# Weight sums and first operands of the feed-forward network moved into the first half of the output projection

## The chip, the cores and the metric

The kernel runs on one core of one Trainium2 chip. The metric is the device time of one execution in microseconds. The core has five engines that run side by side, each through its own queue in order: TensorE (PE, with its weight loads as PEld), VectorE (DVE), ScalarE (ACT), GpSimd (POOL) and SyncE (SP). SP issues most transfers, POOL the others. A difference of under 0.2% (1.45 us here) is about what a measurement of this kernel cannot tell from no change.

## The reference

One decoder layer over 512 tokens of width 1024, all in float32. What matters here are its last two parts:

```python
    merged = jax.nn.sigmoid(gate_a) * y_conv + jax.nn.sigmoid(gate_b) * y_attn
    x = x + merged @ w_out[l]                          # output projection, 1024 x 1024
    h2 = rmsnorm(x, g_ffn[l])
    gu = h2 @ w_ffn_in[l]                              # 1024 x 5632
    x = x + (jax.nn.silu(gu[..., :D_FF]) * gu[..., D_FF:]) @ w_ffn_out[l]
```

Ahead of them stand the input projection, a convolution branch and a forgetting attention (the "mixers").

## The kernel before, in words

Every float32 product is made as three products of split operands: hi·hi, hi·lo and lo·hi, where hi is a cast to the type fp32r (made on ACT) and lo is the rest (a subtraction on DVE, or an accumulating transfer from POOL).

**Output projection.** `n_group` (L263) runs twice, for columns 0 to 511 (`go[0]`) and 512 to 1023 (`go[1]`). Each has four weight chunks of 512 KB, here called chunk 0 to 3 and chunk 4 to 7. Each chunk meets the four token blocks of 128 (t = 0 to 3). A chunk is loaded by SP into `wraw` (3 buffers), cast by ACT into `whi`, and its rest made by DVE into `wlo` (3 buffers each). `go[0]` goes chunk by chunk. `go[1]` takes chunk 4 for all four token blocks and then, for each token block, chunks 5, 6 and 7 (`tail=3`), so that the blocks are done one after the other. `o_done` adds each result to the residual `x1` on DVE and takes the sum of squares on ACT (`junk`). Behind chunk 4's second token block stand the two products of `gain2`, which wait until the first residuals have been added.

**Feed-forward network.** The first product of the network, `w_ffn_in`, is made by a Strassen-Winograd scheme: for each of 11 column groups m there are seven products (m, p), p = 1 to 7, of 128x1024 quarter blocks of weights with operands of the normalised activations. Weight quarters are loaded by SP as `wA` tiles, 512 KB each; from four of them the sums S1 to S4 are made on DVE (`f_sum`, S1 in a tile `wS`, the others in place in `wA`). `w_hi` and `w_lo` make the split `wh` and `wl`. `seq` is the order of the products: (0,1), (0,2), (1,1), (1,2), (0,5), (0,6), (1,5), (0,7), (1,6), (0,4) and so on; products (m,1) and (m,2) need plain quarters, (m,5), (m,6) and (m,7) need sums. A list `todo` says at which step of `seq` each sum and split is made.

**Activations.** `norm2(t)` runs for each token block t: mean square (`ms`), the power on POOL (`rs`), two scalings on DVE (`h`), transposes on PE, copies on ACT (`hr`), and then the splits `bh` (ACT) and `bl` (DVE). For t = 2 and 3 it also makes the Winograd operands: T1 = hr - hr for products (m,5), T2 for (m,6), T3 for (m,7), T4 for (m,4). These steps are handed out by `tokens` between the first products.

**What sets the order.** The program is written in one order by small cooperative threads (`Line.spawn`, `Line.tick`, one tick for each token block of a chunk); each engine works through its own instructions in that order. A thread `prep_first` makes the splits of the first four products and, for m = 0, the four sums and the split of (0,5). It is started ahead of `go[1]`.

**Memory.** A pool `side` holds the mixers' tiles. It is released (`side.release()`) between `go[0]` and `go[1]`, and a new pool takes its place, with 22 buffers `f4` of 4 KB a partition for the network. A transfer into a new tile waits for the last use of whatever lay there. The first eight `wA` loads (m = 0 and 1) are written behind that release, so that in SP's queue they stand behind the last chunk of the output projection.

Of the kernel before, what the change touches and what calls it, by code (L numbers as in the profile page):

```python
# [35 lines left out]
def hybrid_layer(ctx, tc, x, g_mix, w_in, b_forget, w_dw, b_dw, g_ln, b_ln, w_conv_out,  # L36
# [129 lines left out]
    def add_group(w, kt, nk, c0, n, pair=None):  # L166

        first = len(plan)
        for k0 in range(0, kt, nk):
            plan.append(dict(w=w, k0=k0, nk=nk, c0=c0, n=n, pair=pair))  # L170
        return range(first, len(plan))
# [10 lines left out]
    go = [add_group(w_out, KT, 2, c * 512, 512) for c in range(2)]  # L182
# [12 lines left out]
    def load(i):  # L195
        while len(loaded) <= min(i, len(plan) - 1):
            d = plan[len(loaded)]
            n = d["n"]
            cols = n * (1 if d["pair"] is None else 2)
            raw = wp.tile([P, d["nk"], cols], F32, tag="raw", bufs=RAW, name="wraw")  # L200
            for at, c0 in halves(d):
                nc.sync.dma_start(raw[:, :, at:at + n], w_rows(d, c0))
            loaded.append(raw)

    def prepare(i):
        while len(ready) <= min(i, len(plan) - 1):
            load(len(ready))
            raw = loaded[len(ready)]
            loaded[len(ready)] = None
            hi = wp.tile(list(raw.shape), F32R, tag="whi", bufs=3, name="whi")  # L210
            lo = wp.tile(list(raw.shape), F32R, tag="wlo", bufs=3, name="wlo")
            A.copy(hi, raw)  # L212
            if len(ready) in by_dma:

                d = plan[len(ready)]
                A.activation(lo, raw, AF.Copy, scale=-1.0)  # L216
                for at, c0 in halves(d):
                    G.dma_start(lo[:, :, at:at + d["n"]], w_rows(d, c0), accum_op=ALU.add)  # L218
            else:
                V.tensor_tensor(lo, raw, hi.bitcast(F32), op=ALU.subtract)  # L220
            ready.append((hi, lo))

    def chunk(i):
        prepare(i + 2)
        load(i + 2 + RAW)
        d = plan[i]
        return ready[i][0], ready[i][1], d["k0"], d["nk"]

    def mm3(o, l_hi, l_lo, r_hi, r_lo, first, last):
        T.matmul(o, l_hi, r_hi, start=first, stop=False)  # L230
        T.matmul(o, l_hi, r_lo, start=False, stop=False)
        T.matmul(o, l_lo, r_hi, start=False, stop=last)
# [26 lines left out]
    def n_group(group, l_of, done, tail=1, accs=acc):  # L259


        n = plan[group[0]]["n"]
        bank = [accs(n) for _ in range(NT)]  # L263
        k_end = plan[group[-1]]["k0"] + plan[group[-1]]["nk"] - 1

        def one(ch, t):
            hi, lo, k0, nk = ch
            for kk in range(nk):
                l_hi, l_lo = l_of(k0 + kk, t)
                mm3(bank[t], l_hi, l_lo, hi[:, kk, :], lo[:, kk, :], k0 + kk == 0, k0 + kk == k_end)  # L270

        body, last = group[:len(group) - tail], group[len(group) - tail:]
        for i in body:
            ch = chunk(i)
            for t in range(NT):
                one(ch, t)
                Line.tick()
        prepare(last[0] + 2)
        load(last[0] + 2 + RAW)
        chs = [ready[i] + (plan[i]["k0"], plan[i]["nk"]) for i in last]  # L280
        todo = [(t, ch) for t in range(NT) for ch in chs]
        for t, ch in todo:
            one(ch, t)
            if t == NT - 1 and (tail == 1 or ch is not chs[-1]):
                prepare(last[0] + 3 + [c is ch for c in chs].index(True))
            if ch is chs[-1]:
                done(t, bank[t])
            Line.tick()
# [54 lines left out]
    def half(tl, c):  # L343
        return tl[:, c * 512:c * 512 + 512]

    def mean_sq(dst, tl, c):

        junk = wk(BF16, name="junk")
        A.activation(junk, half(tl, c), AF.Square, scale=D ** -0.5, accum_out=dst[:, c:c + 1])
# [489 lines left out]
    norm_th = [None] * NT  # L839

    def o_done(c):
        def done(t, b):
            V.tensor_tensor(half(x1[t], c), half(x1[t], c), b, op=ALU.add)
            mean_sq(ms2[t], x1[t], c)
            if c == 0 and t == 2:
                Line.spawn(gain2(), 4)
            if c == 1:
                norm_th[t] = Line.spawn(norm2(t), 1, order=-t)
        return done

    def gain2():
        for b_ in gain_bcast(row, mx):
            g_bc2.append(slot(name="gffn")[:, :S])
            A.copy(g_bc2[-1], b_)
        yield 0

    m_l = lambda k, t: (merged[k][0][:, t * P:(t + 1) * P], merged[k][1][:, t * P:(t + 1) * P])
    n_group(go[0], m_l, o_done(0), accs=mx)
    Line.join(*m_ths)
    side.release()  # L860

# [15 lines left out]
    def f4(dt=F32, name="f4"):  # L877
        return side.tile([P, KH, 256], dt, tag="f4", bufs=22, name=name)
# [25 lines left out]
    def f_sum(m, key):  # L904
        if key == "S1":
            wq[m, key] = f4(name="wS1")
            V.tensor_tensor(wq[m, key], wq[m, "A21"], wq[m, "A22"], op=ALU.add)
            return
        a, b, o = {"S2": ("S1", "A11", "A11"), "S3": ("A11", "A21", "A21"), "S4": ("A12", "A11", "A12")}[key]
        V.tensor_tensor(wq[m, o], wq[m, a], wq[m, b], op=ALU.subtract)  # L910
# [11 lines left out]
    def w_hi(m, p, alloc=wp4):  # L922
        hi = alloc(F32R, "wh")
        A.copy(hi, wq[m, SRC[p]])  # L924
        ops_.setdefault((m, p), [None, None])[0] = hi

    def w_lo(m, p, alloc=wp4):
        hi, lo = ops_[m, p][0], alloc(F32R, "wl")
        ops_[m, p][1] = lo
        V.tensor_tensor(lo, wq[m, SRC[p]], hi.bitcast(F32), op=ALU.subtract)  # L930
# [11 lines left out]
    def plan_for(m, p, lead, fn, *args):  # L942
        if (m, p) in at:
            todo[max(at[m, p] - lead, 0)].append((fn, args))
# [129 lines left out]
    def prep_first():  # L1074

        yield 0
        for m, p, alloc in ((0, 1, raw4), (0, 2, f4), (1, 1, f4), (1, 2, f4)):
            w_hi(m, p, alloc)
            w_lo(m, p, alloc)
            yield 2  # L1080
        f_sum(0, "S1")
        w_hi(0, 5, raw4)
        yield 1
        f_sum(0, "S3")
        f_sum(0, "S2")
        yield 1
        f_sum(0, "S4")
        w_lo(0, 5, f4)

    def one(n):  # L1090
        product(*seq[n])
# [30 lines left out]
    for m in range(NP):  # L1122
        if m > 1:
            plan_for(m, 2, 5, w_neg, m, 2)
            plan_for(m, 2, 2, w_hi, m, 2)
            plan_for(m, 1, 2, w_hi, m, 1)
            plan_for(m, 1, 2, w_lo, m, 1)
        plan_for(m, 4, 5, w_neg, m, 4)
        plan_for(m, 4, 2, w_hi, m, 4)
        if m > 0:  # L1130
            plan_for(m, 5, 4, f_sum, m, "S1")
            plan_for(m, 5, 4, f_sum, m, "S3")
            plan_for(m, 5, 3, f_sum, m, "S2")
            plan_for(m, 5, 3, f_sum, m, "S4")
        for p in (5, 6, 7, 3):
            if (m, p) != (0, 5):
                plan_for(m, p, 2, w_hi, m, p)
                plan_for(m, p, 2, w_lo, m, p)
    loads = {4: [(2, "A11")], 5: [(2, "A12")], 7: [(2, "A21")], 8: [(2, "A22")], 11: [(3, "A12")], 12: [(3, "A11")]}
    for m in range(2, NP):  # L1140
        loads[at[m, 6] - 2] = [(m + 1, "A21"), (m + 1, "A22")]
        loads[at[m, 7] - 2] = [(m + 2, "A12")]
        loads[at[m, 4] - 2] = [(m + 2, "A11")]

    first_th = Line.spawn(prep_first(), 1)
    n_group(go[1], m_l, o_done(1), tail=3)
    Line.join(first_th, norm_th[0], norm_th[1])
    n2, n3 = (lambda: Line.step(norm_th[2])), (lambda: Line.step(norm_th[3]))
    tokens = {1: (n3, n2, n2), 2: (n3, n3, n2), 3: (n3, n2), 4: (n3, n2), 5: (n3,), 6: (n2, n3)}
    for n in range(NS):  # L1150
# [55 lines left out]
```

## Time and profile before

| | |
|---|---|
| time, median of 3 runs | 724.87 us (723.6 to 725.2) |
| the profiled execution's own time | 724.91 us |
| its span | 723.1 us |
| PE busy | 700.1 us (97%) |
| DVE busy | 461.9 us (64%) |
| ACT busy | 375.0 us (52%) |
| POOL busy | 132.7 us (18%) |
| moved by transfers | 92.13 MB |
| mean granted TensorE clock | 0.994 |

The span is the time from the first to the last instruction in the profile; 1.8 us of the execution lie around it. "Busy" for PE includes time in which matmuls overlap. An engine that waits is shown with the work that released it.

### The profile page before, as it was taken

To read this page: it belongs to the slowest core of one execution; us is meant where nothing else is said; L and a number is where in the kernel's file an instruction comes from. 1 tells how busy PE (TensorE), PEld (TensorE's weight loads), DVE (VectorE), ACT (ScalarE), POOL (GpSimd) and SP (SyncE) were. 2 spreads that over 40 slices of the span, in tenths; PEclk is the share of its full clock that TensorE was granted. 3 is DMA by queue.
4 is the path that set the end of the run, shared out by engine and by line. 5 is a ranking of instruction groups with operands and counts; after the bars stand their busy time and mean duration, and the time that the engine had idled before them with its cause. 6 is when DMAs were issued, how large, how long until landed. Compare 5 with 4: busy or idle time off the path is not lost.

```text
span 723.1 us, 10723 instructions
## 1 busy us (share of the span) xinstructions
PE 700.1 (97%) x4264; PEld 616.7 (85%) x4264; DVE 461.9 (64%) x718; ACT 375.0 (52%) x595; POOL 132.7 (18%) x154
## 2 busy tenths in 40 slices
PE   7999999899999999999887999999999999999997
PEld 5988889778888888887687999999999988888886
DVE  5589968988844567465767666766776664333333
ACT  6423645568877675535366555655556553222320
POOL 1301158633343210400100111111010100000000
PEclk9999999999999999999998999999999999999999
DMA  8438997246556612258003777666677553233203
GB/s 261 98 101 184 181 199 153 73 110 137 121 108 127 145 59 88 89 205 259 1 26 64 176 172 147 158 155 149 154 160 160 88 140 123 88 93 112 87 30 116
DMA packets 67126, 92.13 MB, mean 127 GB/s; under 512 B 3282, under 2 KB 46290, under 8 KB 67076
## 3 DMA queue, kind: packets, MB, share of 16 engines
q1 hardware_dynamic: 48100, 66.11, 30.4%
q0 software_dynamic: 18976, 25.35, 22.0%
q8 instruction: 33, 0.54, 0.3%
q14 instruction: 17, 0.14, 0.1%
HBM read 89.34 MB, written 2.10 MB: 126 GB/s over the span
## 4 chain that ended last, share of the span: by engine, by line
PE 83%; DVE 9%; ACT 4%; issue 1%; DMA 1%; SPq 0%; POOL 0%; ACTq 0%; POOLq 0%; DVEq 0%
PE acc L147 55%; PE mx L147 29%; DVE cv L147 2%; DVE wA L147 1%; DVE x L147 1%; DVE wl L147 1%; ACT wh L924 1%; ACT whi L212 1%; DVE bl L147 1%; DVE wlo L147 1%; DMA x<-in_x_dram 1%; DVE scr L147 1%; DVE h L147 0%; DVE kn L147 0%; DVE hr L147 0%
## 5 line engine op out<-in xcount | busy, mean ns | idle before, releaser
L147 DVE SCALAR_TENSOR_TENSOR cv<-apad,prm,cv 128x512 f32<-128x512 f32 x120 | 87.0, 794 | 0.0
L212 ACT CAST whi<-wraw 128x1024 fp32r<-128x1024 f32 (+1 forms) x52 | 54.4, 1049 | 56.5 <-PE acc L147 35.8
L147 PE MATMUL acc<-hT_hi,whi 128*128 128x512 f32 (+1 forms) x208 | 75.5, 384 | 0.9 <-ACT hT_hi L77 0.7
L147 PE MATMUL acc<-hT_lo,whi 128*128 128x512 f32 (+1 forms) x208 | 73.0, 370 | 0.0
L147 PE MATMUL acc<-hT_hi,wlo 128*128 128x512 f32 (+1 forms) x208 | 72.7, 368 | 0.0
L147 DVE TENSOR_TENSOR wdl<-wd,wdh 128x1024 fp32r<-128x1024 f32 x22 | 27.0, 1225 | 70.1 <-ACT wdh L77 70.1
L147 DVE TENSOR_TENSOR wl<-wA,wh 128x1024 fp32r<-128x1024 f32 x46 | 55.6, 1223 | 22.5 <-ACT wh L924 22.5
L924 ACT CAST wh<-wA 128x1024 fp32r<-128x1024 f32 x66 | 68.0, 1045 | 0.0
L147 PE MATMUL acc<-bl,wh 128*128 128x256 f32 x352 | 57.2, 285 | 4.6 <-DVE bl L147 4.6
L77 ACT CAST wdh<-wd 128x1024 fp32r<-128x1024 f32 x22 | 23.0, 1048 | 74.6 <-PE mx L147 68.3
L920 POOL DMA_DIRECT2D wl<-in_w_ffn_in_dram x20 | 25.7, 1287 | 186.5 <-DVE act L147 91.3
L147 PE MATMUL acc<-bh,wh 128*128 128x256 f32 x352 | 56.9, 284 | 2.1 <-ACT bh L979 0.8
L147 PE MATMUL acc<-bh,wl 128*128 128x256 f32 x352 | 57.2, 285 | 0.2 <-DVE wl L147 0.2
L147 DVE TENSOR_TENSOR wlo<-wraw,whi 128x1024 fp32r<-128x1024 f32 x28 | 34.3, 1224 | 31.6 <-ACT whi L212 30.6
L147 PEld LDWEIGHTS acc<-bl,wh 128*128 128x128 f32 x352 | 48.7, 192 | 5.0 <-DVE bl L147 5.0
L147 PEld LDWEIGHTS acc<-bh,wh 128*128 128x128 f32 x352 | 48.2, 190 | 3.0 <-ACT bh L979 1.2
L147 PEld LDWEIGHTS acc<-bh,wl 128*128 128x128 f32 x352 | 48.6, 191 | 0.5 <-DVE wl L147 0.5
L218 POOL DMA_DIRECT2D wlo<-in_w_in_dram x24 | 29.2, 1215 | 91.0 <-ACT wlo L216 73.9
L147 PEld LDWEIGHTS acc<-hT_hi,whi 128*128 128x128 f32 x208 | 38.1, 193 | 7.1 <-ACT hT_hi L77 1.1
L147 PEld LDWEIGHTS acc<-hT_hi,wlo 128*128 128x128 f32 x208 | 37.6, 189 | 7.2
L147 PE MATMUL mx<-bl,wh 128*128 128x256 f32 x264 | 42.2, 282 | 1.3 <-DVE bl L147 1.3
L147 PE MATMUL acc<-whi,hT_hi 128*128 128x512 f32 (+2 forms) x128 | 43.5, 340 | 0.0
(220 smaller groups left out, 1688.6 us busy)
## 6 DMA issues: line engine op xcount, KB each, us to landing
wA<-in_w_ffn_in_dram SPq DMA_DIRECT2D x44, 512.0 KB, 4.8
wraw<-in_w_in_dram SPq DMA_DIRECT2D x26, 512.0 KB, 3.7
wlo<-in_w_in_dram POOLq DMA_DIRECT2D x22, 512.0 KB, 7.8
wd<-in_w_ffn_out_dram SPq DMA_DIRECT2D x22, 512.0 KB, 3.4
wl<-in_w_ffn_in_dram POOLq DMA_DIRECT2D x20, 512.0 KB, 8.5
wraw<-in_w_in_dram SPq DMA_DIRECT2D x16, 256.0 KB, 4.0
wraw<-in_w_out_dram SPq DMA_DIRECT2D x8, 512.0 KB, 3.4
x<-in_x_dram SPq DMA_DIRECT2D x8, 256.0 KB, 4.4
```

What stands on the lines that cost most here:

```text
L77: A.copy(hi, src)
L147: return f(out, *args, **kw)
L212: A.copy(hi, raw)
L218: G.dma_start(lo[:, :, at:at + d["n"]], w_rows(d, c0), accum_op=ALU.add)
L920: G.dma_start(lo, w_quarter(m, *WHERE[SRC[p]]), accum_op=ALU.add)
L924: A.copy(hi, wq[m, SRC[p]])
```

## The change

The first half of the output projection (`go[0]`) is written behind the release of the mixers' memory and behind the eight `wA` loads, no longer ahead of them. `prep_first` is started ahead of `go[0]`, and it now makes the splits of the first four products and the sums S1 to S4 of both m = 0 and m = 1. Its tiles all come from `f4` (the first product's two came from the `raw` buffers). The split of (0,5) is a thread of its own, `prep_5`, started behind `go[0]`, with both of its tiles from `raw`. The sums of m = 1 are taken out of `todo`.

```diff
     m_l = lambda k, t: (merged[k][0][:, t * P:(t + 1) * P], merged[k][1][:, t * P:(t + 1) * P])
-    n_group(go[0], m_l, o_done(0), accs=mx)
     Line.join(*m_ths)
     side.release()
...
     def prep_first():
         yield 0
-        for m, p, alloc in ((0, 1, raw4), (0, 2, f4), (1, 1, f4), (1, 2, f4)):
-            w_hi(m, p, alloc)
-            w_lo(m, p, alloc)
+        for m, p in ((0, 1), (0, 2), (1, 1), (1, 2)):
+            w_hi(m, p, f4)
+            w_lo(m, p, f4)
             yield 2
-        f_sum(0, "S1")
+        for m in range(2):
+            for key in ("S1", "S3", "S2", "S4"):
+                f_sum(m, key)
+                yield 1
+
+    def prep_5():
+        yield 0
         w_hi(0, 5, raw4)
-        yield 1
-        f_sum(0, "S3")
-        f_sum(0, "S2")
-        yield 1
-        f_sum(0, "S4")
-        w_lo(0, 5, f4)
+        w_lo(0, 5, raw4)
...
-        if m > 0:
+        if m > 1:
             plan_for(m, 5, 4, f_sum, m, "S1")
...
-    first_th = Line.spawn(prep_first(), 1)
+    first_th = Line.spawn(prep_first(), 3)
+    n_group(go[0], m_l, o_done(0), accs=mx)
+    fifth_th = Line.spawn(prep_5(), 6)
     n_group(go[1], m_l, o_done(1), tail=3)
-    Line.join(first_th, norm_th[0], norm_th[1])
+    Line.join(first_th, fifth_th, norm_th[0], norm_th[1])
```

**SP's queue in the output projection.** `wraw` are the chunks of `w_out`, `wA` the weight quarters of the network in the order m = 0, 0, 1, 1, 0, 0, 1, 1. Before:

```order
L202 DMA wraw<-in_w_out_dram 128x2x512 x8
L902 DMA wA_3469<-in_w_ffn_in_dram 128x4x256
L902 DMA wA_3471<-in_w_ffn_in_dram 128x4x256
L902 DMA wA_3473<-in_w_ffn_in_dram 128x4x256
L902 DMA wA_3475<-in_w_ffn_in_dram 128x4x256
L902 DMA wA_3477<-in_w_ffn_in_dram 128x4x256
```

Now:

```order
L202 DMA wraw<-in_w_out_dram 128x2x512 x5
L901 DMA wA_3331<-in_w_ffn_in_dram 128x4x256
L901 DMA wA_3333<-in_w_ffn_in_dram 128x4x256
L901 DMA wA_3335<-in_w_ffn_in_dram 128x4x256
L901 DMA wA_3337<-in_w_ffn_in_dram 128x4x256
L901 DMA wA_3339<-in_w_ffn_in_dram 128x4x256
L901 DMA wA_3341<-in_w_ffn_in_dram 128x4x256
L901 DMA wA_3343<-in_w_ffn_in_dram 128x4x256
L901 DMA wA_3345<-in_w_ffn_in_dram 128x4x256
L202 DMA wraw<-in_w_out_dram 128x2x512 x3
```

The eight loads of the network now stand ahead of chunks 5, 6 and 7 of `w_out`.

**DVE from chunk 4's rest to the first finished token block.** `wlo` are rests of `w_out` chunks, `wl` rests of the network's weights, `wS` and `wA` as outputs are the sums, `x_0` to `x_3` the residual additions of `go[0]` (from `mx`) and `go[1]` (from `acc`). Before (the first row holds chunks 3, 4 and 5):

```order
L147 TENSOR_TENSOR wlo<-wraw,whi 128x1024 x3
L147 TENSOR_TENSOR x_0_3313<-x_0_3313,mx 128x512
L147 TENSOR_TENSOR x_1_3315<-x_1_3315,mx 128x512
L147 TENSOR_TENSOR x_2_3317<-x_2_3317,mx 128x512
L147 TENSOR_TENSOR wlo<-wraw,whi 128x1024
L147 TENSOR_TENSOR x_3_3319<-x_3_3319,mx 128x512
L147 TENSOR_TENSOR wl<-wA_3469,wh 128x1024
L147 TENSOR_TENSOR wl<-wA_3471,wh 128x1024
L147 TENSOR_TENSOR wlo<-wraw,whi 128x1024
L147 TENSOR_TENSOR wl<-wA_3473,wh 128x1024
L147 TENSOR_TENSOR x_0_3313<-x_0_3313,acc 128x512
```

Now, from chunk 4's rest to chunk 6's:

```order
L147 TENSOR_TENSOR wlo<-wraw,whi 128x1024
L147 TENSOR_TENSOR wl<-wA_3337,wh 128x1024
L147 TENSOR_TENSOR wS_3451<-wA_3339,wA_3341 128x1024
L147 TENSOR_TENSOR wA_3339<-wA_3331,wA_3339 128x1024
L147 TENSOR_TENSOR wlo<-wraw,whi 128x1024
L147 TENSOR_TENSOR x_0_3313<-x_0_3313,mx 128x512
L147 TENSOR_TENSOR wA_3331<-wS_3451,wA_3331 128x1024
L147 TENSOR_TENSOR x_1_3315<-x_1_3315,mx 128x512
L147 TENSOR_TENSOR wA_3333<-wA_3333,wA_3331 128x1024
L147 TENSOR_TENSOR x_2_3317<-x_2_3317,mx 128x512
L147 TENSOR_TENSOR wS_3493<-wA_3343,wA_3345 128x1024
L147 TENSOR_TENSOR wlo<-wraw,whi 128x1024
```

Sums of 128x1024 now stand between the residual additions and the rests of chunks 5 and 6; behind the last row follow `x_3`, three more sums, the rest of chunk 7, the rest of (0,5), and only then `x_0` from `acc`. On ACT the casts `wh` stand in the same way between the casts `whi` of the chunks.

**DVE while the token blocks of `go[1]` are finished.** `h` are the scalings of block 0 and then block 1, `x_1` the residual of block 1, `bl` the rest of a network operand. Before:

```order
L147 SCALAR_TENSOR_TENSOR h_3572<-x_0_3313,rs,gffn 128x512
L147 SCALAR_TENSOR_TENSOR h_3573<-x_0_3313,rs,gffn 128x512
L147 TENSOR_TENSOR wS_3582<-wA_3477,wA_3479 128x1024
L147 TENSOR_TENSOR x_1_3315<-x_1_3315,acc 128x512
L147 SCALAR_TENSOR_TENSOR ms<-ms_3322 128x1
L147 TENSOR_TENSOR wA_3477<-wA_3469,wA_3477 128x1024
L147 TENSOR_TENSOR wA_3469<-wS_3582,wA_3469 128x1024
L147 TENSOR_TENSOR bl<-hr,bh 128x4x128
L147 SCALAR_TENSOR_TENSOR h_3618<-x_1_3315,rs,gffn 128x512
L147 SCALAR_TENSOR_TENSOR h_3619<-x_1_3315,rs,gffn 128x512
L147 TENSOR_TENSOR wA_3471<-wA_3471,wA_3469 128x1024
L147 TENSOR_TENSOR wl<-wS_3582,wh 128x1024
```

Now:

```order
L147 SCALAR_TENSOR_TENSOR h_3586<-x_0_3313,rs,gffn 128x512
L147 SCALAR_TENSOR_TENSOR h_3587<-x_0_3313,rs,gffn 128x512
L147 TENSOR_TENSOR x_1_3315<-x_1_3315,acc 128x512
L147 SCALAR_TENSOR_TENSOR ms<-ms_3322 128x1
L147 TENSOR_TENSOR bl<-hr,bh 128x4x128
L147 SCALAR_TENSOR_TENSOR h_3626<-x_1_3315,rs,gffn 128x512
L147 SCALAR_TENSOR_TENSOR h_3627<-x_1_3315,rs,gffn 128x512
```

The four sums and the split of weights are gone from this place. The four sums of m = 1, which stood further on, among the operands T1 and T2, are gone from there too (the line `if m > 1` of the diff).

## Rows read from the trace of the kernel before

**Rows 1.** Stages: us, busy PE PEld DVE ACT POOL, PEclk, DMA share, GB/s

```profile
310.33:332.60 22.27, 22.27 (x98) 18.02 (x97) 12.69 (x17) 8.17 (x14) 0.00 (x0) 1.00 0.65 216
332.60:344.45 11.85, 11.85 (x48) 8.49 (x47) 6.64 (x6) 6.71 (x11) 0.00 (x0) 1.00 0.63 202
344.45:363.21 18.76, 14.66 (x70) 11.20 (x70) 13.23 (x19) 7.40 (x15) 2.50 (x3) 1.00 0.00 1
363.21:381.70 18.49, 17.15 (x140) 16.70 (x140) 13.49 (x20) 10.64 (x18) 0.55 (x1) 1.00 0.09 29
381.70:397.88 16.18, 11.38 (x78) 11.01 (x76) 13.09 (x18) 9.88 (x14) 1.37 (x1) 0.79 0.35 68
397.88:423.00 25.12, 25.12 (x211) 25.12 (x212) 17.12 (x21) 13.26 (x17) 3.60 (x3) 1.00 0.68 167
```

**Rows 2.** PE in order of time, with the idle time before a row

```profile
349.79 0.66 PE L147 MATMUL mx<-ident,h 128*128 128x128 f32 x4 [1.20 <-DVE h L147]
...
357.20 0.66 PE L147 MATMUL mx<-ident,h 128*128 128x128 f32 x4 [2.15 <-DVE h L147]
...
363.21 0.74 PE L147 MATMUL acc<-bh,wh 128*128 128x256 f32 x4 [0.75 <-ACT bh L979]
...
386.42 1.22 PE L147 MATMUL acc<-bl,wh 128*128 128x256 f32 x4 [4.56 <-DVE bl L147]
...
390.75 0.63 PE L147 MATMUL mx<-bh,wh 128*128 128x256 f32 x4
...
393.60 0.70 PE L147 MATMUL acc<-bh,wh 128*128 128x256 f32 x4
...
397.88 0.74 PE L147 MATMUL acc<-bh,wl 128*128 128x256 f32 x4 [0.25 <-DVE wl L147]
```

**Rows 3.** The chain of waits from 344 to 398: start us, us, what

```profile
350.40 1.14 DVE wS L147
...
370.77 0.34 ACT L1054
...
372.07 0.63 ACT c L1054
...
373.21 0.04 DVE hr L147
...
375.10 1.15 DVE wS L147
...
376.27 1.23 DVE wA L147
...
382.17 1.15 DVE wA L147
...
383.34 1.22 DVE wA L147
...
396.69 1.15 DVE wl L147
```

**Rows 4.** DVE in order of time, behind the second product

```profile
370.36 0.69 DVE L147 TENSOR_TENSOR c<-mx,c 128x512 f32<-128x512 f32 x1 [0.26 <-PE mx L147]
```

**Rows 5.** SP, DVE and ACT in order of time, output projection

```profile
307.00 2.10 SPq L202 DMA_DIRECT2D wraw<-in_w_out_dram  x2
...
317.39 1.28 DVE L147 TENSOR_TENSOR mlo<-gate,mhi 128x512 fp32r<-128x512 f32 x2
...
341.40 1.23 DVE L147 TENSOR_TENSOR wlo<-wraw,whi 128x1024 fp32r<-128x1024 f32 x1 [0.93 <-ACT whi L212]
...
327.07 1.05 ACT L212 CAST whi<-wraw 128x1024 fp32r<-128x1024 f32 x1 [4.48 <-PE mx L147]
```

**Rows 6.** Busy time by stage, the transfers' share and rate (columns as in rows 1)

```profile
312.00:314.00 2.00, 2.00 (x10) 1.60 (x9) 1.97 (x4) 0.64 (x2) 0.00 (x0) 1.00 0.95 367
334.00:336.00 2.00, 2.00 (x8) 1.21 (x8) 1.59 (x2) 0.37 (x1) 0.00 (x0) 1.00 1.09 348
338.00:340.00 2.00, 2.00 (x10) 1.61 (x9) 1.30 (x2) 1.21 (x2) 0.00 (x0) 1.00 0.80 256
```

## The prediction

> **What bounds the kernel now.** I read the stages first, then PE in order of time with its waits, then the chain of waits. In the stages the reader sees PE without a gap through both halves of the output projection up to 344.45 us, and again from 397.88 us on; between them lie three stages in which it is busy 14.66 of 18.76, 17.15 of 18.49 and 11.38 of 16.18 us [rows 1]. So the 53.4 us from 344.45 to 397.88 are what can be won, at most the 10.24 us of idle time in them and what the clock lost in the last. PE's own rows name the releasers: 1.20 and 2.15 us for `h` from DVE, 0.75 us for `bh`, 4.56 us for a `bl` of operand T2, 0.25 us for a `wl` [rows 2]; one more wait, 1.33 us for a `bl` of T1, is the idle time of the second stage, 18.49 less 17.15. The chain of waits then shows what was late: apart from the first product it does not run through PE at all here, but through DVE and ACT, and among its steps are the sums that the change moves [rows 3]. DVE has several jobs here, and the activations wait behind the weights in its queue.
>
> **The change, step by step.** I make the sum against the profiled execution, 724.91 us (span 723.1), which is the median of the runs shown, 724.87, to 0.04 us.
>
> *What leaves the stretch after 344.45.* One `wl`, the four sums of m = 0 and the rest of (0,5) leave the place between the residual additions, the scalings and `bl`. With them gone, DVE holds at that place only short work. Each of the three waits is shorter than the weight work that stood in its path: 1.20 us against a rest of 1.23, 2.15 against three sums of 1.15, 0.75 against a sum and a rest of together some 2.3 [rows 2, 3, 5]. I therefore let all three go whole: 4.10 us, the difference of 18.76 and 14.66 [rows 1, 2]. The first product starts at 359.1, not 363.21. The cover is PE's own work on the next block; were it gone, the three waits would come back for what the residual, the square and the power take, which I can't bound from these rows but by the 4.10.
>
> *The table load.* Behind the second product DVE adds `c` from 370.36 for 0.69 us, to 371.05 [rows 4]. ACT could then take its silu, but a table load that began at 370.77, when the `bh` ahead of it was done, holds it until 372.07 [rows 3]. That `bh` hangs on `x_3` and the scaling of block 3, which DVE reached late. In the new order block 3's residual is added as soon as PE delivers it, so the table load is over before `c` is added: 372.07 less 371.09, 0.98 us.
>
> *The sums of m = 1.* From the subtraction at 373.21 to the `wl` at 397.84 the chain runs through DVE and ACT without PE: 24.63 us. Four sums lie in it, 1.15 + 1.23 + 1.15 + 1.22 = 4.75 us [rows 3]. They leave; what else is in this chain keeps its order on both engines. The chain takes 19.88 us.
>
> Sum: 4.10 + 0.98 + 4.75 = 9.83 us. Four restarts of PE cost a little besides (a first group of four takes 0.74 us against 0.63 [rows 2]); I take **9.9 us**: 724.9 - 9.9 = **715.0 us**. After the `wl` at 397.84 PE waits for nothing in the next 25 us [rows 1], and all loads and splits there hang on tiles that PE or ACT gives free, so the lead should be kept to the end.
>
> *What PE still waits for.* From 359.1 to the end of that `wl`, 397.84 - 9.8 = 388.0, lie 28.9 us, and PE has eight products of 2.85 us (390.75 to 393.60 [rows 2]), two thirds of a ninth and two groups of transposes to do, some 26.3. So PE will still wait 2.6 us there for what the chain makes: for T2's `bl`, for `wh` and `wl` of (1,5) and (1,6), for the copy that frees (0,7)'s bank. That is the chain's length seen from PE, and it is in the sum.
>
> *Where the work goes.* From 310.33 to 344.45 DVE is busy 12.69 + 6.64 = 19.33 of 34.12 us [rows 1]. Ten more operations of 128x1024 come into this stretch (one `wl`, eight sums, the rest of (0,5)); at 1.23 us each [rows 5] that is 12.3 us, together 31.6. It fits with 2.5 us to spare, so PE's unbroken work covers them, provided that the operands are there in time. ACT has 14.88 of 34.12 and gets two casts more.
>
> *The loads.* SP reaches the first three `wA` loads behind chunk 4's issue, at 307.00 + 2.10 = 309.1 us [rows 5], no longer behind chunk 7. The fourth must wait for the last `mlo`, in the row at 317.39 [rows 5], because it takes the memory of a gate tile; a `wlo` of 1.23 us that stood ahead of it now stands behind it, so it comes at about 316.5. Queued behind it on SP are the other four `wA` loads and chunks 5, 6 and 7. Until 314 the transfers are taken by other loads [rows 6]; from then on nine loads, eight quarters and chunk 5, have to pass: 9 x 0.524 = 4.72 MB. At the 348 GB/s at which the same eight loads ran together [rows 6] this takes 13.6 us: chunk 5 is there at 327.6. In the run of before its cast started at 327.07 [rows 5], when PE gave a buffer free. It is 0.5 us late.
>
> *Who waits for it.* Behind `wlo` of chunk 5 on DVE stand six sums and the rest of chunk 6 at 1.15 us [rows 3], four residual additions at up to 0.69 [rows 4], and, by my estimate, 0.4 of waiting for chunk 6's cast: 11.2 us. Then comes the rest of chunk 7. Cast by 328.6, `wlo` by 329.9: DVE is free for chunk 7 at 341.1. Its row is at 341.40, after 0.93 us of waiting [rows 5]. PE's 48 matmuls take 11.85 us [rows 1]; the last six begin at 343.0 and read this rest first at 343.2, and it is ready at 342.6. So chunk 5 may be late by another 0.9 us before PE waits (343.2 less 1.23 less 341.1), and the price of the move is nothing. That is the lower end; the upper end is each microsecond beyond, one for one.
>
> [...]
>
> **The rivals.**
> [...]
>
> *Half of the sums were covered (717.4 us).* The last two sums stand behind a `wl` that itself waited for ACT; if ACT's `bh` and `wh` set the pace there, only two of the four count: 715.0 + 2.4. Against it: the chain runs through all four.
>
> *Chunk 5 comes late (718.9 us).* If the nine loads move at 256 GB/s, the rate at the end of the eight [rows 6], they take 18.4 us: chunk 5 at 332.4, 4.8 us later than reckoned, 0.9 of it free: 715.0 + 3.9. For it: these loads now share the queues with the residual's loads and the chunks.
>
> *The same delay, past the turning point (728.8 us, slower).* At the 167 GB/s of the stage behind 397.88 [rows 1] the nine loads take 28.3 us, chunk 5 lands at 342.3, 14.7 us late, and PE stands for 13.8 us in the output projection: 715.0 + 13.8. It decides from 9.9 + 0.9 = 10.8 us of lateness on, that is below 4.72 MB in 24.4 us, 193 GB/s. Against it: 348 GB/s in the same loads; the 167 belong to a stage in which the transfers were busy only 0.68 of the time.
>
> *It does nothing (723.5 us or more).* The loads near 200 GB/s would just give the gain back.
>
> **How the numbers follow.** The forecast 0.70 (its own range 713.9 to 716.5), the clock 0.10, the covered sums 0.07, the late chunk 0.06, nothing 0.02, the far too late chunk 0.05. Faster by over 0.2% (under 723.4; 0.2% is about what a measurement of this kernel can tell) are the first four, 0.93; same 0.02; slower 0.05. The range from 712.5 to 718.9 holds the first three and the edge of the fourth, some 0.85 to 0.9; its low end is the forecast less the 1.5 us of the clock and 1.0 for restarts and waits that I let stand in the chain, its high end chunk 5 at 256 GB/s.
>
> **What would show it.** Right: first `wA` load near 309, the fourth near 316.5; chunk 5's cast within a microsecond or two of 327; no idle PE up to 344.5; transposes without a wait and the first product near 359; a silu that does not follow a table load; the subtraction of T1's second half near 368, the `wl` of (1,6) ended near 388; idle PE between 344 and 398 of some 3 us in waits of under 1 us, clock 1.00. Wrong: PE waiting for `x`, `wlo` or `whi` ahead of 344; waits for `h` that stay though DVE is empty, which would put them on ACT's squares or POOL's power; a chain that is shorter but a PE end that is not, which would put a new wait behind 398, on a load of m = 2 or an accumulating transfer.

## The result and the profile after

The changed kernel takes 716.57 us in the median (713.33 to 716.75, 4 runs) beside 725.04 us for the kernel before on the same chip (723.6 to 727.12): ratio 0.9873, 95% interval 0.9841 to 0.9905. On two further occasions it took 717.02 us beside 726.30 (0.9873, 0.9858 to 0.9888) and 715.03 us beside 726.34 (0.9848, 0.983 to 0.9866). The gain is 8.5 to 11.3 us, where 9.9 was forecast. The profiled execution is the fastest one, 713.33 us with a span of 711.5 us; why it is 3.2 us under the median is taken up below (the changed kernel again).

The stages, the first two cut as in [rows 1], the others at the first product, at the subtraction and at PE's row behind the `wl` of (1,6) (columns: us, busy PE PEld DVE ACT POOL, PEclk, DMA share, GB/s):

```profile
310.33:332.60 22.27, 22.27 (x98) 18.03 (x97) 19.43 (x23) 10.89 (x14) 0.00 (x0) 1.00 0.88 305
332.60:344.45 11.85, 11.85 (x47) 8.19 (x46) 10.81 (x11) 5.75 (x11) 0.00 (x0) 1.00 0.00 1
344.45:357.87 13.42, 13.42 (x69) 11.05 (x68) 7.72 (x15) 6.74 (x14) 1.66 (x3) 1.00 0.00 1
357.87:366.55 8.68, 8.68 (x75) 8.68 (x74) 4.35 (x9) 5.38 (x11) 0.55 (x1) 1.00 0.00 0
366.55:386.39 19.84, 18.14 (x144) 17.12 (x142) 15.79 (x23) 14.26 (x21) 1.37 (x1) 1.00 0.37 82
386.39:411.51 25.12, 25.12 (x211) 25.12 (x212) 17.12 (x21) 13.31 (x17) 3.62 (x3) 1.00 0.67 167
```

PE now has no gap from 310.33 to 366.55 us, loses 1.70 us up to 386.39, and the clock is at its upper level (1.00) throughout. DVE is busy 30.24 of 34.12 us in the first two rows (19.33 before [rows 1]). The last row, cut to the length of the last one of before, holds the same 211 matmuls; from its start to the end of the span it is 325.1 us, before 325.2: the lead is kept. PE in order of time, against [rows 2]:

```profile
347.80 0.60 PE L147 MATMUL mx<-ident,h 128*128 128x128 f32 x4
...
352.83 0.60 PE L147 MATMUL mx<-ident,h 128*128 128x128 f32 x4
...
357.87 0.63 PE L147 MATMUL acc<-bh,wh 128*128 128x256 f32 x4
...
374.97 0.74 PE L147 MATMUL acc<-bl,wh 128*128 128x256 f32 x4 [0.39 <-DVE bl L147]
...
378.13 0.74 PE L147 MATMUL mx<-bh,wh 128*128 128x256 f32 x4 [0.52 <-ACT wh L923]
...
382.07 0.74 PE L147 MATMUL acc<-bh,wh 128*128 128x256 f32 x4 [0.52 <-ACT c L1056]
...
386.39 0.74 PE L147 MATMUL acc<-bh,wl 128*128 128x256 f32 x4 [0.22 <-DVE wl L147]
```

The three waits ahead of the first product are gone, the one for T1's `bl` too, and the 4.56 us for T2's `bl` are 0.39. The chain of waits, against [rows 3]:

```profile
364.69 0.70 DVE c L147
...
366.55 0.69 DVE hr L147
...
385.20 1.15 DVE wl L147
386.35 0.04 issue
386.39 3.70 PE acc L147 x29
```

From the subtraction to the end of the `wl` of (1,6) it is 19.80 us, where it was 24.63. ACT in order of time shows that no table load stands between the addition of `c` and the silu any more:

```profile
363.72 1.28 ACT L1053 ACT_TABLE_LOAD   x1
365.41 0.63 ACT L1053 ACTIVATE c<-c 128x512 f32<-128x512 f32 x1 [0.41 <-DVE c L147]
```

Against before, from the first residual addition of `go[1]` (DVE at 344.47 before, 343.84 now): to the first product 18.74 us are now 14.03; to the addition of `c` 7.15 are 6.82; to the subtraction 2.85 are 1.86; from there to PE's row behind the `wl` 24.67 are 19.84. Together **10.86 us** less.

The loads, against [rows 5] (SP, ACT, DVE and PE in order of time):

```profile
308.26 9.89 SPq L901 DMA_DIRECT2D wA<-in_w_ffn_in_dram  x8
318.25 5.10 SPq L202 DMA_DIRECT2D wraw<-in_w_out_dram  x3
...
327.62 1.05 ACT L212 CAST whi<-wraw 128x1024 fp32r<-128x1024 f32 x1 [4.96 <-PE mx L147]
...
341.11 1.22 DVE L147 TENSOR_TENSOR wlo<-wraw,whi 128x1024 fp32r<-128x1024 f32 x1
...
342.38 0.50 PE L147 MATMUL acc<-wlo,mhi 128*128 128x512 f32 x1
```

The third row is the cast of chunk 5 (the profile puts its wait down to PE; in the two other profiles of this kernel it names the transfer), the fourth the rest of chunk 7, the fifth PE's first use of it. The rest ends at 342.33 and PE reads it at 342.38, 0.37 us behind the row ahead of it where unbroken rows follow each other after 0.23: it came 0.1 us late, almost in time.

### The profile page after: what moved, and what is told of

It is laid out like the page before. It is cut to its first block, busy times and chain, and to the rows that moved or that the text cites. A ratio compares the mean times of both kernels' runs of the same rounds, so it can differ in the third digit from the quotient of the medians.

```text
span 711.5 us, 10727 instructions
## 1 busy us (share of the span) xinstructions
PE 696.4 (98%) x4264; PEld 613.3 (86%) x4264; DVE 461.6 (65%) x718; ACT 375.5 (53%) x595; POOL 131.9 (19%) x154
## 4 chain that ended last, share of the span: by engine, by line
PE 87%; DVE 7%; ACT 3%; issue 1%; DMA 1%; SPq 0%; POOL 0%; ACTq 0%; DVEq 0%
PE acc L147 57%; PE mx L147 30%; DVE cv L147 2%; DVE x L147 1%; ACT whi L212 1%; DVE wl L147 1%; ACT wh L923 1%; DVE wlo L147 1%; DMA x<-in_x_dram 1%; DVE bl L147 1%; DVE scr L147 1%; DVE kn L147 0%; DVE hr L147 0%; DVE wA L147 0%; ACT p L662 0%
## 5 line engine op out<-in xcount | busy, mean ns | idle before, releaser
L147 PE MATMUL acc<-wlo,hT_hi 128*128 128x512 f32 (+2 forms) x128 | 43.4, 339 | 0.0
L147 PE MATMUL acc<-whi,hT_lo 128*128 128x512 f32 (+2 forms) x128 | 43.4, 339 | 0.0
```

Of the source, the lines that this page charges most:

```text
L147: return f(out, *args, **kw)
```

## The experiments

In the profiled executions the first 20 us differ, mostly because the same rows of PE go there at two paces, 1.21 or 2.07 to 2.08 us for the first eight matmuls of 128x256 (last section). To compare them I count from the first row of a single matmul behind the start-up (23.91 us in the kernel before) to the end of the span:

| kernel | that row at | span | from there to the end | median, beside before |
|---|---|---|---|---|
| before | 23.91 | 723.1 | 699.2 | |
| changed | 22.68 | 711.5 | 688.8 | 716.57, 725.04 |
| changed, again | 25.29 | 714.9 | 689.6 | 717.02, 726.30 |
| changed, third time | 22.27 | 712.4 | 690.1 | 715.03, 726.34 |
| loads only | 24.79 | 724.4 | 699.6 | 725.99, 726.30 |
| m = 0 early | 25.28 | 718.8 | 693.5 | 720.04, 726.30 |
| m = 1 early | 23.93 | 719.3 | 695.4 | 721.65, 726.30 |
| chunk 5 first | 24.25 | 715.1 | 690.9 | 715.06, 725.81 |
| chunk 5 first, again | 24.30 | 714.8 | 690.5 | 715.07, 726.34 |
| four loads more | 25.21 | 721.3 | 696.1 | 722.94, 725.81 |
| eight loads more | 24.22 | 725.6 | 701.4 | 728.17, 725.81 |
| before, wait filled | 25.55 | 725.0 | 699.5 | 726.26, 725.81 |

So like for like the change is worth 9.1 to 10.4 us. This count has a spread of its own: the first cast of an output projection chunk, at 304.67 us in the kernel before and behind code that no edit touches, lies 280.7 to 281.8 us behind that row in the twelve profiles. Counted from that cast to the end, the three profiles of the changed kernel are 9.8 to 10.7 us shorter than before, the loads alone 0.3 us longer, m = 0 early 6.1 and m = 1 early 4.0 us shorter, and the kernel before with its wait filled the same.

**The changed kernel again.** No edit.

> The changed kernel again, unedited. Its profiled execution took 713.33 us, the other four 716.5 to 716.75. Step sum: the gain sits between 344 and 398 us of the kernel before (some 10.9 us in the profiled execution); in an execution of 716.6 us the same stretch should be as short, and the 3.3 us should show as PE idle at one other place. Late-chunk theory: that place is the output projection, with chunk 5's cast at 330 us or later and PE waiting for whi or wlo ahead of 344 us. Rival: the 3.3 us lie outside the changed code (ahead of 300 us or behind 400 us). Median expected 716.6, 715.9 to 717.2.

717.02 us (716.58 to 717.48). The start-up costs this execution 2.61 us against the profiled one above. The other difference is in the output projection (ACT, DVE and PE in order of time):

```profile
330.93 1.05 ACT L212 CAST whi<-wraw 128x1024 fp32r<-128x1024 f32 x1 [5.75 <-DMA wraw<-in_w_out_dram]
...
344.42 1.22 DVE L147 TENSOR_TENSOR wlo<-wraw,whi 128x1024 fp32r<-128x1024 f32 x1
...
345.69 0.50 PE L147 MATMUL acc<-wlo,mhi 128*128 128x512 f32 x1 [0.76 <-DVE wlo L147]
```

Chunk 5's cast waits for its transfer, DVE comes to chunk 7's rest 13.49 us behind it (13.49 in the first profile, too), and PE waits 0.76 us. Counted from the start-up's end the cast is at 305.64, where it was at 304.94: 0.70 us later, and so is PE's first use of chunk 7's rest (320.40 against 319.70). 2.61 + 0.70 = 3.31, and the spans differ by 3.4. So the rival and the late-chunk theory both hold in part: most of the difference lies ahead of the changed code, the rest where chunk 5 is late. The other executions of some 716.5 us have no profile; that they differ in the same way is likely, but not shown.

**The loads alone.** The release and the eight loads stay ahead of `go[0]`; all work is where it was before.

```diff
-    first_th = Line.spawn(prep_first(), 3)
     n_group(go[0], m_l, o_done(0), accs=mx)
-    fifth_th = Line.spawn(prep_5(), 6)
+    first_th = Line.spawn(prep_first(), 1)
     n_group(go[1], m_l, o_done(1), tail=3)
```

`prep_first` and `todo` are those of before.

> The memory is released and the eight loads are issued ahead of the first half of the output projection, as in the change; all splits and sums stand where they stood before. Step sum: no wait in the kernel before was for a wA load, so this alone gives nothing: 725, 724.2 to 725.8, with the waits of 1.2, 2.2, 0.8, 1.3 and 4.6 us all there. Loads theory (the early loads are the gain): about 717. Late-chunk theory: chunk 5 behind eight loads costs some 3 us: 727 to 728.

725.99 us, ratio 1.0002 (0.9993 to 1.0012). The waits of 1.19, 2.16, 0.74, 1.33 and 4.56 us are all there. Early operands are worth nothing by themselves. Chunk 5's cast waits 6.97 us for its transfer here (at 330.54 us, 2.5 us later than before, counted from the first cast), and PE does not wait for its rest or chunk 7's: without the sums in DVE's queue this lateness is covered. (The expected 725 was reckoned from the 724.9 us of the first occasion; the kernel before takes 726.30 here.)

**The work of m = 0 alone.** The sums of m = 1 stay in `todo`.

```diff
-        for m in range(2):
+        for m in range(1):
...
-        if m > 1:
+        if m > 0:
             plan_for(m, 5, 4, f_sum, m, "S1")
```

> The change without its last part: the sums of m = 1 stay in the todo list, among the operands T1 and T2. Step sum: it keeps 4.10 + 0.98 us and some tenths for restarts, and loses 4.75: about 4.75 above the changed kernel, 721.3 (720.5 to 722). Covered-sums rival: only two of the four sums count, 2.4 above the changed kernel, 719.0. In the profile the waits ahead of the first product are gone and the waits of 1.3 and 4.6 us for bl stay.

720.04 us, ratio 0.9913 (0.9899 to 0.9926); counted from the start-up 3.9 us behind the changed kernel's second execution and 4.7 behind its first. PE's waits behind the first product:

```profile
374.53 0.74 PE L147 MATMUL mx<-bl,wh 128*128 128x256 f32 x4 [0.35 <-DVE bl L147]
...
382.19 0.79 PE L147 MATMUL acc<-bl,wh 128*128 128x256 f32 x4 [4.56 <-DVE bl L147]
...
393.60 0.74 PE L147 MATMUL acc<-bh,wl 128*128 128x256 f32 x4 [0.23 <-DVE wl L147]
```

The row that reads T1's rest is, in the kernel before:

```profile
378.76 0.74 PE L147 MATMUL mx<-bl,wh 128*128 128x256 f32 x4 [1.33 <-DVE bl L147]
```

The three waits ahead of the first product are gone, and T1's is 0.35 instead of 1.33: 0.98 us less, as much as was reckoned for the table load. T2's 4.56 us are untouched. From the row that reads T1's rest to the last row shown it is 19.07 us, in the kernel before, from 378.76 to 397.88 [rows 2], 19.12: the m = 1 sums still cost what they did. The median lies under the range that I gave for the step sum (720.5 to 722), 3.0 us above the changed kernel on the same chip and not 4.75. Part of that is that without these sums DVE is early in the output projection and PE's 0.76 us for chunk 7's rest go as well (4.75 - 0.76 = 3.99, as in the profiles); the remaining 1.0 us is no more than the interval of these five runs.

**The sums of m = 1 alone.** They are made in `go[0]`, the work of m = 0 stays behind it. Since they are made in place ahead of the splits of (1,1) and (1,2), these two products take sums instead of the plain quarters, so the output is not the layer's; operations and sizes are the same.

```diff
+    def prep_sums():
+        yield 0
+        for key in ("S1", "S3", "S2", "S4"):
+            f_sum(1, key)
+            yield 2
...
+    sums_th = Line.spawn(prep_sums(), 9)
     n_group(go[0], m_l, o_done(0), accs=mx)
+    first_th = Line.spawn(prep_first(), 1)
```

> Only the sums of m = 1 are made in the first half of the output projection; the splits of the first four products and the sums of m = 0 stand where they stood before. Step sum: the waits of 1.20, 2.15 and 0.75 us stay, the chain behind the second product loses 4.75 us: 720.2 (719.5 to 721). Covered-sums rival: 722.6. Were both parts needed together, nothing: 725.

721.65 us, ratio 0.9937 (0.9925 to 0.995). PE's waits:

```profile
344.01 0.50 PE L147 MATMUL acc<-wlo,mhi 128*128 128x512 f32 x1 [0.50 <-DVE wlo L147]
...
364.20 0.74 PE L147 MATMUL acc<-bh,wh 128*128 128x256 f32 x4 [0.76 <-ACT bh L978]
...
382.62 0.74 PE L147 MATMUL acc<-bl,wh 128*128 128x256 f32 x4 [1.37 <-DVE bl L147]
...
394.09 0.74 PE L147 MATMUL acc<-bh,wl 128*128 128x256 f32 x4 [0.25 <-DVE wl L147]
```

The waits ahead of the first product stay. DVE's subtraction is at 374.20, and the last row 19.89 us behind it (24.67 before): all four sums come out of the chain, 4.8 us, and 0.5 us are lost in the output projection. The median is over the range that I gave, 719.5 to 721, which was reckoned from 724.9; it is 4.65 us under the 726.30 of the kernel before on this chip. The two halves give 5.7 and 3.8 us by the table, 9.5 together, as the whole change does: neither needs the other. By the medians of this chip they give 6.26 and 4.65, together 1.6 us more than the 9.28 of the whole, at the edge of what these few runs can tell from nothing.

**Chunk 5 first.** Chunk 5's load ahead of the last two weight loads.

```diff
     for m, key in ((0, "A11"), (0, "A12"), (1, "A11"), (1, "A12"), (0, "A21"), (0, "A22"), (1, "A21"), (1, "A22")):
+        if (m, key) == (1, "A21"):
+            load(go[1][1])
         f_load(m, key)
```

> The changed kernel with chunk 5's load moved ahead of the last two weight loads (m = 1) in SP's queue; the same transfers, the same work on every engine. Theory (chunk 5's landing sets the end of DVE's work ahead of 344 us, and its slack is already used up: in the second profile of the changed kernel its cast at 330.93 waits for the transfer and PE then waits 0.76 us for the rest of chunk 7): the cast is released by PE or comes at least 1.4 us earlier against PE's rows, the wait of 0.76 us goes, and the time is some 0.8 us under the 717.0 of the unedited kernel: 716.2. Rival (the last two loads are now late instead, or DVE has no room): a wait for a sum or a rest takes its place, 717.0 or more.

715.06 us (712.12 to 716.93), ratio 0.9849 (0.9827 to 0.9871). The cast of chunk 5 at 328.50 is released by PE, and no wait for a rest is left. But the span is no shorter like for like. Stages of 2 us (columns as above):

```profile
340.00:342.00 2.00, 2.00 (x6) 1.52 (x5) 1.97 (x2) 0.13 (x1) 0.00 (x0) 0.50 0.00 0
342.00:344.00 2.00, 2.00 (x7) 1.59 (x6) 0.07 (x1) 0.85 (x1) 0.00 (x0) 0.66 0.00 0
```

PE, busy throughout, runs here at its lower level (0.50): eight matmuls stand 0.43 us apart instead of 0.23, which costs 1.6 us. I ran it beside the unedited kernel:

> The changed kernel unedited, beside the next one on the same chip. Theory: 716.6 to 717.0, with a wait of up to 0.8 us for the rest of chunk 7 in the output projection.

> The changed kernel with chunk 5's load ahead of the last two weight loads, a second time, beside the unedited one on the same chip. Theory (0.76 us of waiting for chunk 7's rest goes): 0.5 to 1.0 us under the run beside it, 716.0 or so, and a profile in which chunk 5's cast is released by PE. Rival (the median of 715.06 was only a matter of where the clock rose): the same as the run beside it within 0.4 us.

715.03 us unedited (here, too, its profile has a wait of 0.85 us for chunk 7's rest; the median is below what I expected) and 715.07 with chunk 5 first. The wait goes and the medians show no time won; with four and five runs that spread over 2.6 and 2.3 us they could not tell 0.76 us from nothing. The second profile of this order has the slow clock at the same place again (0.50 from 340 to 342 us), and in both profiles a first stretch at the lower level lies at 132 to 135 us (0.50 from 132 to 134), ahead of anything edited. The order does not bring the slow clock about by itself: the mean clock of the two profiled executions, 716.93 and 716.54 us, is 0.995, and three others of the same order have 1.000, at 712.12, 715.06 and 715.70 us. What does stays open; in the two profiles the start-up ended near 24.3 us, in those of the unedited kernel at 22.3, 22.7 and 25.3.

**More loads.** The last four weight loads are issued a second time, or a second and a third time, into the same tiles, ahead of chunk 5.

```diff
+    for m, key in ((0, "A21"), (0, "A22"), (1, "A21"), (1, "A22")) * 1:
+        nc.sync.dma_start(wq[m, key], w_quarter(m, *WHERE[key]))
```

> The changed kernel with the last four weight loads issued a second time into the same tiles (2.10 MB more ahead of chunks 5, 6 and 7). Theory (slack used up, then one for one): at the 350 to 400 GB/s of the profile the four take 5.3 to 6.0 us, chunk 5's cast comes that much later and the time is 722.3 to 723.0. With the 0.9 us of slack that the prediction gave it: 721.4 to 722.1. Rival (the transfers are hidden, PE waits for DVE's amount of work and not for chunk 5): 717.0.

> The same with the last four weight loads issued three times (4.19 MB more ahead of chunk 5). Theory, one for one: 10.5 to 12.0 us more than the 717.0 of the changed kernel, 727.5 to 729.0, so slower than the kernel before (726.3 on this chip): the whole gain is given back by late loads. Rival (hidden, or covered in part): 717 to 722.

Four more: 722.94 us, ratio 0.9956 (0.9943 to 0.997). Eight more: 728.17 us, 1.0027 (1.0015 to 1.0039), slower than before. ACT and PE with four more,

```profile
337.07 1.04 ACT L212 CAST whi<-wraw 128x1024 fp32r<-128x1024 f32 x1 [11.66 <-DMA wraw<-in_w_out_dram]
...
340.02 1.12 PE L147 MATMUL mx<-grow,onesr 1*128 1x512 f32 x2 [2.76 <-DVE x L147]
```

and with eight more:

```profile
341.60 1.04 ACT L212 CAST whi<-wraw 128x1024 fp32r<-128x1024 f32 x1 [17.78 <-DMA wraw<-in_w_out_dram]
...
344.56 3.80 PE L147 MATMUL mx<-grow,onesr 1*128 1x512 f32 x4 [8.88 <-DVE x L147]
```

Against the second execution of the changed kernel and counted from the start-up, chunk 5's cast is 6.22 and 11.74 us later, and the end 6.5 and 11.8 us. One for one, from the first microsecond on: there is no slack left. PE now stands at the products of `gain2`, since the residual additions wait behind chunk 5's rest in DVE's queue. These waits, 3.37 (2.76 and one more of 0.61) and 8.88 us, are shorter than the lateness, because PE is then at its lower level (0.50), at 342 to 348 and 340 to 353 us, which takes up what would have been a second wait, for the rest of chunk 7. That rest ends at 351.77 and 356.31 us, and PE first reads it at 351.83 and 356.53: DVE's chain behind chunk 5 still sets the time, with at most 0.2 us from the slow clock.

**The long wait filled.** The kernel before, with 34 matmuls of a tile of zeros in PE's wait for T2's `bl`.

```diff
             for w in range(3):
+                if (m, p, f, w) == (0, 6, 0, 1):
+                    for _ in range(34):
+                        T.matmul(o[:, :256], zero, bh[:, 0, :], start=False, stop=False, skip_group_check=True)
```

> The kernel before, with 34 matmuls of a tile of zeros (128x128 by 128x256, adding nothing) between the first and the second group of four of product (0,6), where PE waits 4.56 us for the rest of T2; PE has some 4 us of them to do in that wait. Theory (the slow clock behind the wait is not on the path, since the chain on DVE and ACT arrives later anyway): the clock stays at its upper level behind the wait, PE waits longer for the wl of (1,6) instead (1.5 us and more, not 0.25), and the time stays at 726.3. Rival (the clock counts): 1.5 us faster, 724.8.

726.26 us, ratio 1.0003 (0.9992 to 1.0013). PE in order of time:

```profile
383.59 4.24 PE L147 MATMUL acc<-bh,zero 128*128 128x256 f32 x34
388.32 0.74 PE L147 MATMUL acc<-bl,wh 128*128 128x256 f32 x4 [0.48 <-DVE bl L147]
...
391.52 0.74 PE L147 MATMUL mx<-bh,wh 128*128 128x256 f32 x4 [0.55 <-ACT wh L924]
...
399.78 0.74 PE L147 MATMUL acc<-bh,wl 128*128 128x256 f32 x4 [0.25 <-DVE wl L147]
```

The clock now stays at 1.00 behind the wait (0.50 before), PE has done (0,6) 2.65 us behind T2's rest (390.97) instead of 4.33, and gives the time back in waits of 0.55, 0.51 (for the copy that frees a bank, at 395.46) and 0.25 us and in the rows that restart behind them. From T2's rest to the last row it is 11.46 us, as before ([rows 2]: 386.42 to 397.88). I had put the whole loss into the last wait; the place was wrong, the sum right. The slow clock there was not on the path. The same profile has one more stretch at the lower level, at 359 to 363 us (0.50 from 360 to 362), that the profile before has not: the first product comes 0.66 us later by it (6.67 us behind the transposes at 359.09; in the profile before 6.01 us behind those at 357.20), but T1's rest is read 21.56 us behind them in both, after a wait of 1.02 instead of 1.33. There it is not on the path either.

## Why the prediction was right

The forecast was 715.0 us, the medians on three occasions are 715.03, 716.57 and 717.02 (two of them just over the forecast's own range, 713.9 to 716.5), and the terms of the sum hold one by one, but for two small ones that were mis-sized in opposite directions.

- *The three waits, 4.10 us.* All gone, with PE unbroken up to the first product. The stretch from the first residual addition is 4.71 us shorter.
- *The restarts, taken as "a little".* Mis-sized: 0.61 us in that stretch and 0.33 in the first two products, 0.9 together where I added 0.07. The rows of before bear it out: the last matmul ahead of the wait at 349.79 begins 1.59 us before that row, which is 0.39 besides the wait where unbroken rows follow each other after 0.24, and the row itself takes 0.42 us to the next instead of 0.35, together some 0.2 us for one restart.
- *The table load, 0.98 us.* 0.99 (2.85 to 1.86), and 0.98 in T1's wait with m = 0 alone.
- *The sums of m = 1, 4.75 us.* The chain is 19.80 us where I worked out 19.88. The rival in which half of them were covered falls by the chain and by the run with m = 1 alone.
- *Early loads bring nothing themselves.* 1.0002 by the run with the loads alone.
- *DVE's room.* 30.24 us busy of 34.12, I had 31.6.
- *Chunk 5.* The step that was mis-sized in the other direction. I had its landing at 327.6, 0.5 us late, and 0.9 us more to spare. Counted from the first cast of the output projection (304.67 us before), its casts began at 328.5, 329.3 and 329.4 in the three profiles of the changed kernel: 0.9, 1.7 and 1.8 us later than reckoned. The chain behind it was right (13.49 us from cast to chunk 7's rest; I had 13.5), and so was the spare time: PE waited 0.1, 0.76 and 0.85 us, which is what lies beyond 0.9. That took back about what the restarts gave. What was too small is the amount that passes ahead of the chunk. The transfers, from the 314 us of the prediction to chunk 5's cast (the first and the second profile, columns as above):

```profile
313.11:327.62 14.51, 14.51 (x65) 11.74 (x64) 12.82 (x13) 7.56 (x9) 0.00 (x0) 1.00 1.07 360
315.62:330.93 15.31, 15.31 (x68) 12.40 (x67) 12.91 (x13) 7.58 (x9) 0.00 (x0) 1.00 1.08 362
```

These are 5.2 and 5.5 MB at 360 and 362 GB/s, where I had 4.72 MB at 348: the rate was better than reckoned, the amount 0.5 to 0.8 MB larger. The fourth `wA` load was issued at 315.6 us in the first profile, 316.5 by the count of before, as reckoned. Which loads the rest belongs to is not separated; the first `wA` loads were issued while other loads ran, and chunk 6 right behind chunk 5, chunk 7 at 323.0. The far end of this rival is real: with 11.7 us more lateness the kernel is slower than before, as the step with its turning point of 10.8 us said.
- *The clock.* The 1.5 us at the low end of the range are the difference of 4.33 us (386.42 to 390.75, granted clock 0.51) and 2.85 us (390.75 to 393.60, 1.00) for six groups each [rows 2]; no run shows them as time won. In their place the run with the wait filled showed a clock of 1.00 behind the wait and 726.26 us beside 725.81 for the kernel before. In the first profile of the changed kernel the clock behind the wait is 1.00, too, and its 713.33 us are 1.7 us under the forecast; by the run with the wait filled the clock is not the cause. What made that execution fast is the start-up, 1.23 us shorter than in the profile of before, and chunk 5 almost in time.
- *What PE still waits for.* 1.70 us between 366.55 and 386.39, where I had 2.6: for T2's `bl`, a `wh`, a copy and a `wl`, as named.

The start-up was in no term. It ends between 22.27 and 25.55 us in the twelve profiles, of either kernel, and carries most of why the first profile lies 1.7 us under the forecast and the second, 716.63 us, 1.6 us over it: 22.68 and 25.29 us against 23.91, which is 1.2 less and 1.4 more.

## What to carry to other kernels

Work that an in-order engine does for later stages cost little in a stage where the matmuls are unbroken, and cost its whole length in a chain that runs through that engine: the sums and rests fit among the output projection's matmuls, and were worth 4.8 us of chain and 4.1 us of waits behind it. What such a move really spent here is the order of the loads: the spare time of the last weight chunks, after which every microsecond of transfer ahead of chunk 5 was a microsecond of the kernel. Before a profile is compared with another, find the first row behind the start-up, or better the last row ahead of the edited code, and count from there.

## What the runs showed of the hardware

**The pace of PE's first rows moved whole executions.** PE's first rows in the changed kernel's first and second profile:

```profile
11.90 1.21 PE L147 MATMUL acc<-hT_hi,whi 128*128 128x256 f32 x8 [0.68 <-ACT hT_hi L77]
...
22.68 0.28 PE L147 MATMUL acc<-hT_hi,whi 128*128 128x256 f32 x1
```

```profile
12.47 2.08 PE L147 MATMUL acc<-hT_hi,whi 128*128 128x256 f32 x8 [0.67 <-ACT hT_hi L77]
...
25.29 0.28 PE L147 MATMUL acc<-hT_hi,whi 128*128 128x256 f32 x1
```

The same eight matmuls take 1.21 us in the first and 2.08 in the second, though the granted clock of both is given as 1.00 from 0 to 20 us. Of the 2.61 us between these two executions 0.57 lie ahead of these rows, where PE waits once more for `x` in the second, and 2.04 behind them. The kernel before and the third profile of the changed one begin this row at the same moment, 11.50 us, take 2.07 and 1.21 us for it, and come out of the start-up at 23.91 and 22.27. Over all profiles the row behind the start-up lies between 22.27 and 25.55 us. What sets the pace these rows do not show.

**The clock fell also where PE was busy.** With chunk 5 first it went to 0.50 at 340 us some 1.2 us behind the four products of `gain2` (operands 1x512, 1.98 us), without a wait of PE near it. In the unedited kernel's three profiles it did not, at the same place. With eight loads more, where PE waited 8.88 us up to 344.56, it was at 0.50 from 340 to 353 us. What decides it in the first case I did not find out.

**Loads of 512 KB, many of them queued, moved at some 360 GB/s.** With four and eight loads more, the transfers moved 359 and 356 GB/s from 316 us to chunk 5's cast. The extra loads made the cast 6.22 and 11.74 us later, 2.10 MB at 337 GB/s and 4.19 MB at 357 GB/s.
